# Attention with exponentiated scores as the stationary operand of the value product, plain fp32 loads with casts on GpSimd, and a hand-written order

## Chip, cores and metric

The kernel runs on one core of a Trainium2 chip. The metric is the device time of one execution in microseconds (us), taken as the median of several runs; every run quoted as fast lies within 1.5% of the fastest of its kernel. The profile is of one execution; its span is about 2 us shorter than the time of the same run.

## The reference

```python
q, k, v: float32 [8, 8, 512, 64]      # batch, heads, sequence, dim
scores = einsum('bhqd,bhkd->bhqk', q, k) / sqrt(64)
attn   = exp(scores - scores.max(-1)) ; attn = attn / attn.sum(-1)
out    = einsum('bhqk,bhkd->bhqd', attn, v)      # float32
```

There are 64 heads. Both kernels treat two at a time ("a pair", 32 in all), leave out the subtraction of the maximum (the exponent is of moderate size for these inputs), and get the sum for the normalization from a 65th column of ones beside the 64 of the values.

## The kernel before

The scores are computed transposed: 128 keys on the partitions, 512 queries along the free axis. "A half" below is half of a pair's work: two of its four key blocks, for both heads, which is two exponentials of 1,024 elements per partition. PSUM tiles are marked with the space that they take.

```python
q16, k16 = bt[b]                       # fp16; loaded a batch at a time by casting GpSimd DMAs
vp = apool.tile([P, 2, NI, D + 1], FP16, ...)            # values, and a column of ones
...                                    # 4 VectorE copies into qkp, two heads side by side
for i in range(NI):                    # 8 transposes into tqk_ps (2 KiB), one copy to tqk
    nc.tensor.transpose(tqk_ps[:, 0, i, :], qkp[:, 0, i, :], ident16)
    nc.tensor.transpose(tqk_ps[:, 1, i, :], qkp[:, 1, i, :], ident16)
...
for half in range(2):
    st_ps = [pspool.tile([P, 2, S], FP32, tag="ps_st", bufs=2, ...) for h01 in range(2)]   # 2 x 4 KiB
    for cc in range(2):
        for h01 in range(2):           # scores: 64 rows of the array for each head
            nc.tensor.matmul(st_ps[h01][:, cc, :], tqk[po:po+64, 1, c*P:(c+1)*P], tqk[po:po+64, 0, :], ...)
    for h01 in range(2):
        nc.scalar.activation(out=pt[h01][:, 2*half:2*half+2, :], in_=st_ps[h01][:, :, :], func=EXP, scale=scale)

ot_ps = [pspool.tile([P, S], FP32, tag="ps_ot", bufs=2, ...) for h01 in range(2)]          # 2 x 2 KiB
for h01 in range(2):
    for c in range(NI):                # values stationary (65 columns), exponentials moving (512)
        nc.tensor.matmul(ot_ps[h01][0:D+1, :], vp[:, h01, c, :], pt[h01][:, c, :], ...)
    nc.vector.tensor_copy(out=ot_sb[0:D+1, h01, :], in_=ot_ps[h01][0:D+1, :])
    op_ps = pspool.tile([P, NI, D + 1], FP32, tag="ps_outp", bufs=1, ...)                  # up to 2 KiB
    for c in range(NI):                # four fp32 transposes put the queries back on partitions
        nc.tensor.transpose(op_ps[:, c, :], ot_sb[0:D+1, h01, c*P:(c+1)*P], ident32[0:D+1, 0:D+1])
    ...                                # reciprocal of column 65, multiply, store on the sync queue
```

Counted in units of 2 KiB per partition, called banks below, the tiles above take 4 + 2 + 1 + 1 = 8 banks, 16 KiB.

The softmax here doesn't subtract the row's maximum and nothing guards it: scores larger than these inputs give would overflow.

## Time and profile before

| | before |
|---|---|
| time, median of 3 runs | 190.99 us (190.87 to 191.46) |
| span of the profile | 189.0 us |
| TensorE (PE) / ScalarE (ACT) / VectorE (DVE) busy | 88% / 66% / 61% |

In the page's second part each digit is the busy share of one of 40 slices of the span, in tenths:

```profile
PE   0057999999999999999999999999999999999980
ACT  2014388688786868686886868686877868686860
```

TensorE is at nine tenths or more from the fifth slice on, and ScalarE alternates between 6 and 8. (In these views PEld is TensorE's loading of stationary operands, POOL is GpSimd, and PEclk is the clock that TensorE was granted.) Groups of instructions are listed as line, engine, operation, output<-input, count, then busy time, mean ns of one, and the idle time just before it with what ended it. Two of TensorE's groups:

```profile
L110 PE MATMUL st<-tqk 64*128 64x512 f16 x256 | 65.6, 386 | 3.6 <-DVE tqk L98 0.8
...
L148 PE MATMUL outp<-ident,otsb 65*128 65x65 f32 x256 | 27.4, 229 | 3.2 <-DVE outsb L154 1.4
```

The second is the group of fp32 transposes that exist only because the value product leaves its output with queries on the free axis. The two DMA queues (packets, MB, share of 16 engines):

```profile
q0 software_dynamic: 50432, 12.59, 70.2%
q1 hardware_dynamic: 8704, 8.39, 12.8%
```

### The profile page before, as it was taken

Reading aid. Unit: us, or ns where it says so; the run is one execution under the profiler, and the core shown is the slowest. Engines: PE = TensorE matmul, PEld = TensorE weight load, DVE = VectorE, ACT = ScalarE, POOL = GpSimd, SP = SyncE. Lnnn points to the kernel's source line nnn. Section 1 sums busy time; section 2 is a strip of 40 time slices with the busy share of each in tenths; the row PEclk is TensorE's granted clock in tenths of the full one; section 3 lists DMA queues with packets and bytes.
Section 4 is the critical chain, followed back from the end, with each engine's and each line's share of the span. In section 5 each row is a group of like instructions: output and inputs, shape, how many; then the busy total and the mean of one; then the engine's idle time right before and its main releaser. Section 6 shows DMA issues by size and latency. Waiting matters only on the chain.

```text
span 189.0 us, 2952 instructions
## 1 busy us (share of the span) xinstructions
PE 166.8 (88%) x1024; PEld 74.9 (40%) x1024; DVE 115.1 (61%) x352; ACT 125.2 (66%) x129; POOL 66.5 (35%) x120
## 2 busy tenths in 40 slices
PE   0057999999999999999999999999999999999980
PEld 0033433434444343544353443434353443434330
DVE  0255455675859486666759585766757594656462
ACT  2014388688786868686886868686877868686860
POOL 7482643423453335413543336304133333300000
PEclk9999999999999999999999999999999999999999
DMA  3999999965599578995699478996555463631111
GB/s 42 191 182 183 129 156 189 179 87 77 65 147 196 80 91 111 182 170 83 86 143 188 74 91 126 179 149 87 83 83 76 34 90 67 87 69 59 55 57 55
DMA packets 59150, 21.16 MB, mean 112 GB/s; under 512 B 34560, under 2 KB 59136, under 8 KB 59136
## 3 DMA queue, kind: packets, MB, share of 16 engines
q0 software_dynamic: 50432, 12.59, 70.2%
q1 hardware_dynamic: 8704, 8.39, 12.8%
q8 instruction: 8, 0.13, 0.3%
q14 instruction: 6, 0.05, 0.1%
HBM read 25.17 MB, written 8.39 MB: 178 GB/s over the span
## 4 chain that ended last, share of the span: by engine, by line
PE 68%; DVE 11%; ACT 9%; DMA 6%; issue 2%; POOL 2%; ACTq 1%; POOLq 0%
PE st L110 31%; PE ot L131 31%; ACT pt L118 9%; DMA k<-in_k_dram 6%; DVE otsb L140 5%; DVE tqk L98 5%; PE outp L148 4%; PE tqkps L95 1%; POOL q L49 1%; ACTq L190 0%; POOL k L54 0%; DVE outsb L154 0%; DVE qkp L88 0%; POOL ident masks.py:199 0%; PE tqkps L96 0%
## 5 line engine op out<-in xcount | busy, mean ns | idle before, releaser
L118 ACT ACTIVATE pt<-st 128x1024 f16<-128x1024 f32 x128 | 124.0, 1024 | 56.8 <-PE st L110 56.8
L131 PE MATMUL ot<-pt,vp 128*65 128x512 f16 x256 | 73.4, 390 | 0.3 <-ACT pt L118 0.3
L140 DVE COPY otsb<-ot 65x512 f32<-65x512 f32 x64 | 43.8, 685 | 43.5 <-PE ot L131 43.5
L110 PE MATMUL st<-tqk 64*128 64x512 f16 x256 | 65.6, 386 | 3.6 <-DVE tqk L98 0.8
L77 POOL DMA_DIRECT2D vp<-in_v_dram x64 | 47.2, 743 | 14.4 <-POOL vp L75 9.6
L131 PEld LDWEIGHTS <-vp 128*65 128x65 f16 x256 | 21.9, 111 | 41.5 <-issue 33.9
L148 PEld LDWEIGHTS outp<-ident,otsb 65*128 65x128 f32 x256 | 23.4, 141 | 17.8 <-DVE otsb L140 9.3
L148 PE MATMUL outp<-ident,otsb 65*128 65x65 f32 x256 | 27.4, 229 | 3.2 <-DVE outsb L154 1.4
L75 POOL MEMSET vp<- 128x8 f16 x32 | 4.0, 139 | 70.6 <-PE ot L131 70.6
L95 PE MATMUL tqkps<-ident,qkp 128*128 128x128 f16 x128 | 21.0, 231 | 8.7 <-DVE qkp L84 7.6
L154 DVE TENSOR_TENSOR outsb<-outp,rcp 128x256 f32<-128x256 f32 x64 | 27.0, 422 | 1.3
L110 PEld LDWEIGHTS <-tqk 64*128 64x128 f16 x256 | 13.3, 94 | 25.7 <-issue 16.6
L96 PE MATMUL tqkps<-ident,qkp 128*128 128x128 f16 x128 | 20.9, 230 | 2.8 <-DVE qkp L88 2.8
L98 DVE COPY tqk<-tqkps 128x1024 f16<-128x1024 f16 x32 | 21.4, 670 | 0.5 <-PE tqkps L96 0.5
L84 DVE COPY qkp<-q 128x256 f16<-128x256 f16 x64 | 15.6, 256 | 8.4 <-DMA q<-in_q_dram 8.4
L153 DVE RECIPROCAL rcp<-outp 128x4 f32<-128x4 f32 x64 | 11.2, 175 | 14.5 <-PE outp L148 14.2
L95 PEld LDWEIGHTS <-qkp 128*128 128x128 f16 x128 | 12.8, 102 | 18.3 <-issue 7.6
L88 DVE COPY qkp<-k 128x256 f16<-128x256 f16 x64 | 16.4, 275 | 2.7 <-DMA k<-in_k_dram 2.7
L96 PEld LDWEIGHTS <-qkp 128*128 128x128 f16 x128 | 13.2, 103 | 6.9 <-DVE qkp L88 2.9
L49 POOL DMA_DIRECT2D q<-in_q_dram x8 | 7.2, 902 | 12.6 <-DVE qkp L88 9.2
L54 POOL DMA_DIRECT2D k<-in_k_dram x8 | 7.1, 892 | 0.1
L118 ACT ACT_TABLE_LOAD x1 | 1.3, 1283 | 0.7 <-PEq L179 0.7
(6 smaller groups left out, 1.3 us busy)
## 6 DMA issues: line engine op xcount, KB each, us to landing
out_dram<-outsb SPq DMA_DIRECT2D x32, 256.0 KB, 2.4
q<-in_q_dram POOLq DMA_DIRECT2D x8, 512.0 KB, 6.6
k<-in_k_dram POOLq DMA_DIRECT2D x8, 512.0 KB, 8.2
vp<-in_v_dram POOLq DMA_DIRECT2D x64, 64.0 KB, 3.1
```

Source lines behind the costliest of these rows:

```text
L77: nc.gpsimd.dma_start(out=vp[:, h01, :, 0:D], in_=v[b, hA + h01].rearrange("(p i) d -> p i d", i=NI),)
L84: nc.vector.tensor_copy(out=qkp[:, 0, :, 64 * h01 : 64 * h01 + 64], in_=q16[:, hA + h01, :].rearrange("p (i d) -> p i d", d=D),)
L88: nc.vector.tensor_copy(out=qkp[:, 1, :, 64 * h01 : 64 * h01 + 64], in_=k16[:, hA + h01, :].rearrange("p (i d) -> p i d", d=D),)
L95: nc.tensor.transpose(tqk_ps[:, 0, i, :], qkp[:, 0, i, :], ident16)
L96: nc.tensor.transpose(tqk_ps[:, 1, i, :], qkp[:, 1, i, :], ident16)
L98: nc.vector.tensor_copy(out=tqk[:, :, :], in_=tqk_ps[:, :, :, :])
L110: nc.tensor.matmul(st_ps[h01][:, cc, :], tqk[po : po + 64, 1, c * P : (c + 1) * P], tqk[po : po + 64, 0, :], start=True, stop=True,)
L118: nc.scalar.activation(out=pt[h01][:, 2 * half : 2 * half + 2, :], in_=st_ps[h01][:, :, :], func=EXP, scale=scale,)
L131: nc.tensor.matmul(ot_ps[h01][0 : D + 1, :], vp[:, h01, c, :], pt[h01][:, c, :], start=(c == 0), stop=(c == NI - 1),)
L140: nc.vector.tensor_copy(out=ot_sb[0 : D + 1, h01, :], in_=ot_ps[h01][0 : D + 1, :])
L148: nc.tensor.transpose(op_ps[:, c, :], ot_sb[0 : D + 1, h01, c * P : (c + 1) * P], ident32[0 : D + 1, 0 : D + 1],)
L154: nc.vector.tensor_tensor(out=out_sb[:, h01, :, :], in0=op_ps[:, :, 0:D], in1=rcp[:, h01, :].broadcast_to([P, NI, D]), op=AluOp.mult,)
```

## The change

Three things are changed at once. The value product is turned round, so that a 128x128 block of exponentials is the stationary operand and 65 columns of values move past it; queries then land on partitions, and the transposes back and their evictions go. The casting loads on GpSimd's queue become plain fp32 loads on the sync queue, with copies to fp16 on GpSimd. The order of instructions is written by hand, one pair ahead, in place of the framework's scheduler. The score buffers go from two to three, and the output from 2 + 1 PSUM tiles to one.

```diff
+    ps_st = ctx.enter_context(tc.tile_pool(name="ps_st", bufs=3, space=bass.MemoryType.PSUM))
+    ps_o = ctx.enter_context(tc.tile_pool(name="ps_o", bufs=1, space=bass.MemoryType.PSUM))
+    ps_t = ctx.enter_context(tc.tile_pool(name="ps_t", bufs=1, space=bass.MemoryType.PSUM))
 ...                                   (load: k, q and v of a pair, one transfer each)
-            nc.gpsimd.dma_start(
-                out=vp[:, h01, :, 0:D],
-                in_=v[b, hA + h01].rearrange("(p i) d -> p i d", i=NI),
+            nc.sync.dma_start(
+                out=t.rearrange("p h i d -> p h (i d)"),
+                in_=src[b, h : h + 2].rearrange("h (p i) d -> p h (i d)", i=NI),
             )
 ...                                   (cast: three per pair)
+            nc.gpsimd.tensor_copy(
+                out=t[:, n].rearrange("p i (h d) -> p h i d", h=2),
+                in_=tiles[name][:, :, :, :],
+            )
 ...                                   (values)
-            for c in range(NI):
-                nc.tensor.matmul(
-                    ot_ps[h01][0 : D + 1, :],
-                    vp[:, h01, c, :],
-                    pt[h01][:, c, :],
+        for qc in range(NI):
             for c in range(NI):
                 nc.tensor.matmul(
+                    o[:, qc, :],
+                    pts[g][h][:, c, qc * P : (qc + 1) * P],
+                    vps[g % NV][:, h, c, :],
                     start=(c == 0),
                     stop=(c == NI - 1),
                 )
-        for h01 in range(2):
-            nc.vector.tensor_copy(out=ot_sb[0 : D + 1, h01, :], in_=ot_ps[h01][0 : D + 1, :])
 ...                                   (fp32 transposes back: removed)
+    with tc.manual_schedule():
 ...                                   (5 pairs loaded, 3 cast)
+        for g in range(2):
+            transpose(g, 1)
+            transpose(g, 0)
+            if g == 0:
+                scores(0, 0)
+                scores(0, 1)
+        transpose(2, 1)
+        transpose(2, 0)
+        for g in range(NP):
+            load(g + AHEAD)
+            cast(g + 3)
+            scores(g + 1, 0)
+            values(g, 0)
+            transpose(g + 3, 1)
+            scores(g + 1, 1)
+            values(g, 1)
+            transpose(g + 3, 0)
```

More of the change, by code (lines that the diff above doesn't have):

```diff
@@ L4 @@
 import concourse.tile as tile
-from concourse import bass_utils, mybir
+from concourse import mybir
 from concourse._compat import with_exitstack
@@ L30 @@
     scale = float(D) ** -0.5
-    n_pairs = (B * H) // 2
+    NP = (B * H) // 2
     ppb = H // 2
-    cpool = ctx.enter_context(tc.tile_pool(name="att_const", bufs=1))
-    bpool = ctx.enter_context(tc.tile_pool(name="att_batch", bufs=2))
-    apool = ctx.enter_context(tc.tile_pool(name="att_a", bufs=4))
-    ppool = ctx.enter_context(tc.tile_pool(name="att_pair", bufs=3))
-    hpool = ctx.enter_context(tc.tile_pool(name="att_head", bufs=4))
-    opool = ctx.enter_context(tc.tile_pool(name="att_out", bufs=3))
@@ L41 @@
-    pspool = ctx.enter_context(tc.tile_pool(name="att_psum", bufs=1, space=bass.MemoryType.PSUM))
-    bt = {}
-    ident16 = None
-    ident32 = None
-    def batch_load(b):
-        q16 = bpool.tile([P, H, NI * D], FP16, tag="q16", name=f"q16_{b}")
-        nc.gpsimd.dma_start(
-            out=q16.rearrange("p h (i d) -> p h i d", d=D),
-            in_=q[b].rearrange("h (p i) d -> p h i d", i=NI),
-        )
-        k16 = bpool.tile([P, H, NI * D], FP16, tag="k16", name=f"k16_{b}")
-        nc.gpsimd.dma_start(
-            out=k16.rearrange("p h (i d) -> p h i d", d=D),
-            in_=k[b].rearrange("h (p i) d -> p h i d", i=NI),
-        )
-        bt[b] = (q16, k16)
@@ L60 @@
-    batch_load(0)
-    ident16 = cpool.tile([P, P], FP16, name="ident16")
-    make_identity(nc, ident16)
-    ident32 = cpool.tile([P, P], FP32, name="ident32")
-    make_identity(nc, ident32)
-    for g in range(n_pairs):
-        b = g // ppb
-        gl = g % ppb
-        hA = 2 * gl
-        if gl == 0 and b + 1 < B:
-            batch_load(b + 1)
-        q16, k16 = bt[b]
-        vp = apool.tile([P, 2, NI, D + 1], FP16, tag="vp", name=f"vp_{g}")
-        nc.gpsimd.memset(vp[:, :, :, D : D + 1], 1.0)
-        for h01 in range(2):
-            nc.gpsimd.dma_start(
-                out=vp[:, h01, :, 0:D],
-                in_=v[b, hA + h01].rearrange("(p i) d -> p i d", i=NI),
-            )
-        qkp = apool.tile([P, 2, NI, P], FP16, tag="qkp", name=f"qkp_{g}")
-        for h01 in range(2):
-            nc.vector.tensor_copy(
-                out=qkp[:, 0, :, 64 * h01 : 64 * h01 + 64],
-                in_=q16[:, hA + h01, :].rearrange("p (i d) -> p i d", d=D),
-            )
-            nc.vector.tensor_copy(
-                out=qkp[:, 1, :, 64 * h01 : 64 * h01 + 64],
-                in_=k16[:, hA + h01, :].rearrange("p (i d) -> p i d", d=D),
-            )
-        tqk_ps = pspool.tile([P, 2, NI, P], FP16, tag="ps_tqk", bufs=1, name=f"tqkps_{g}")
-        for i in range(NI):
-            nc.tensor.transpose(tqk_ps[:, 0, i, :], qkp[:, 0, i, :], ident16)
-            nc.tensor.transpose(tqk_ps[:, 1, i, :], qkp[:, 1, i, :], ident16)
-        tqk = ppool.tile([P, 2, S], FP16, tag="tqk", name=f"tqk_{g}")
-        nc.vector.tensor_copy(out=tqk[:, :, :], in_=tqk_ps[:, :, :, :])
-        pt = [hpool.tile([P, NI, S], FP16, tag="pt", name=f"pt_{g}_{h}") for h in range(2)]
-        for half in range(2):
-            st_ps = [
-                pspool.tile([P, 2, S], FP32, tag="ps_st", bufs=2, name=f"st_{g}_{h01}_{half}")
-                for h01 in range(2)
-            ]
-            for cc in range(2):
-                c = 2 * half + cc
-                for h01 in range(2):
-                    po = 64 * h01
-                    nc.tensor.matmul(
-                        st_ps[h01][:, cc, :],
-                        tqk[po : po + 64, 1, c * P : (c + 1) * P],
-                        tqk[po : po + 64, 0, :],
-                        start=True,
-                        stop=True,
-                    )
-            for h01 in range(2):
-                nc.scalar.activation(
-                    out=pt[h01][:, 2 * half : 2 * half + 2, :],
-                    in_=st_ps[h01][:, :, :],
-                    func=EXP,
-                    scale=scale,
-                )
-        ot_ps = [
-            pspool.tile([P, S], FP32, tag="ps_ot", bufs=2, name=f"ot_{g}_{h01}")
-            for h01 in range(2)
-        ]
-        for h01 in range(2):
@@ new lines @@
+    cpool = ctx.enter_context(tc.tile_pool(name="const", bufs=1))
+    lpool = ctx.enter_context(tc.tile_pool(name="load", bufs=6))
+    qpool = ctx.enter_context(tc.tile_pool(name="qk16", bufs=3))
+    tpool = ctx.enter_context(tc.tile_pool(name="tqk", bufs=4))
+    ppool = ctx.enter_context(tc.tile_pool(name="pt", bufs=6))
+    opool = ctx.enter_context(tc.tile_pool(name="out", bufs=4))
+    ps_st = ctx.enter_context(tc.tile_pool(name="ps_st", bufs=3, space=bass.MemoryType.PSUM))
+    ps_o = ctx.enter_context(tc.tile_pool(name="ps_o", bufs=1, space=bass.MemoryType.PSUM))
@@ new lines, with where, load @@
+    ps_t = ctx.enter_context(tc.tile_pool(name="ps_t", bufs=1, space=bass.MemoryType.PSUM))
+    NV = 6
+    vps = [cpool.tile([P, 2, NI, D + 1], FP16, name=f"vp{n}") for n in range(NV)]
+    ident = cpool.tile([P, P], FP16, name="ident")
+    raw = {}
+    qkp = {}
+    tqk = {}
+    st = {}
+    pts = {}
+    outs = {}
+    def where(g):
+        return g // ppb, 2 * (g % ppb)
+    def load(g):
+        if g >= NP:
+            return
+        b, h = where(g)
+        tiles = {}
+        for name, src in (("k", k), ("q", q), ("v", v)):
+            t = lpool.tile([P, 2, NI, D], FP32, tag=f"{name}32", name=f"{name}32_{g}")
+            nc.sync.dma_start(
+                out=t.rearrange("p h i d -> p h (i d)"),
+                in_=src[b, h : h + 2].rearrange("h (p i) d -> p h (i d)", i=NI),
+            )
+            tiles[name] = t
+        raw[g] = tiles
@@ new lines, in cast, with transpose @@
+    def cast(g):
+        if g >= NP:
+            return
+        tiles = raw.pop(g)
+        t = qpool.tile([P, 2, NI, P], FP16, tag="qkp", name=f"qkp_{g}")
+        for n, name in ((1, "k"), (0, "q")):
+            nc.gpsimd.tensor_copy(
+                out=t[:, n].rearrange("p i (h d) -> p h i d", h=2),
+                in_=tiles[name][:, :, :, :],
+            )
+        qkp[g] = t
+        nc.gpsimd.tensor_copy(out=vps[g % NV][:, :, :, 0:D], in_=tiles["v"][:, :, :, :])
+    def transpose(g, n):
+        if g >= NP:
+            return
+        if n == 1:
+            tqk[g] = tpool.tile([P, 2, S], FP16, tag="tqk", name=f"tqk_{g}")
+        tp = ps_t.tile([P, NI, P], FP16, tag="tp", name=f"tp_{g}_{n}")
+        for i in range(NI):
+            nc.tensor.transpose(tp[:, i, :], qkp[g][:, n, i, :], ident)
+        nc.vector.tensor_copy(out=tqk[g][:, n, :], in_=tp.rearrange("p i c -> p (i c)"))
@@ new lines, in scores @@
+    def scores(g, half):
+        if g >= NP:
+            return
+        if half == 0:
+            pts[g] = [
+                ppool.tile([P, NI, S], FP16, tag="pt", name=f"pt_{g}_{h}") for h in range(2)
+            ]
+        ss = [ps_st.tile([P, 2, S], FP32, tag="st", name=f"st_{g}_{h}_{half}") for h in range(2)]
+        for cc in range(2):
+            c = 2 * half + cc
+            for h in range(2):
+                po = 64 * h
+                nc.tensor.matmul(
+                    ss[h][:, cc, :],
+                    tqk[g][po : po + 64, 1, c * P : (c + 1) * P],
+                    tqk[g][po : po + 64, 0, :],
+                    start=True,
+                    stop=True,
+                )
+        for h in range(2):
+            nc.scalar.activation(
+                out=pts[g][h][:, 2 * half : 2 * half + 2, :],
+                in_=ss[h][:, :, :],
+                func=EXP,
+                scale=scale,
+            )
@@ L130, with values @@
+    def values(g, h):
+        if g < 0:
+            return
+        if h == 0:
+            outs[g] = opool.tile([P, 2, NI, D], FP32, tag="ob", name=f"ob_{g}")
+        ob = outs[g]
+        o = ps_o.tile([P, NI, D + 1], FP32, tag="o", name=f"o_{g}_{h}")
+        for qc in range(NI):
             for c in range(NI):
                 nc.tensor.matmul(
-                    ot_ps[h01][0 : D + 1, :],
-                    vp[:, h01, c, :],
-                    pt[h01][:, c, :],
+                    o[:, qc, :],
+                    pts[g][h][:, c, qc * P : (qc + 1) * P],
+                    vps[g % NV][:, h, c, :],
@@ L137 @@
                 )
-        ot_sb = opool.tile([P, 2, S], FP32, tag="ot_sb", name=f"otsb_{g}")
-        for h01 in range(2):
-            nc.vector.tensor_copy(out=ot_sb[0 : D + 1, h01, :], in_=ot_ps[h01][0 : D + 1, :])
-        out_sb = opool.tile([P, 2, NI, D], FP32, tag="out_sb", name=f"outsb_{g}")
-        rcp = opool.tile([P, 2, NI], FP32, tag="rcp", name=f"rcp_{g}")
-        for h01 in range(2):
-            op_ps = pspool.tile([P, NI, D + 1], FP32, tag="ps_outp", bufs=1,
-                                name=f"outp_{g}_{h01}")
-            for c in range(NI):
-                nc.tensor.transpose(
-                    op_ps[:, c, :],
-                    ot_sb[0 : D + 1, h01, c * P : (c + 1) * P],
-                    ident32[0 : D + 1, 0 : D + 1],
-                )
-            nc.vector.reciprocal(out=rcp[:, h01, :], in_=op_ps[:, :, D : D + 1])
-            nc.vector.tensor_tensor(
-                out=out_sb[:, h01, :, :],
-                in0=op_ps[:, :, 0:D],
-                in1=rcp[:, h01, :].broadcast_to([P, NI, D]),
-                op=AluOp.mult,
-            )
@@ L161 @@
-        nc.sync.dma_start(
-            out=out[b, hA : hA + 2].rearrange("h (p i) d -> p h (i d)", i=NI),
-            in_=out_sb[:, :, :, :],
-        )
+        rc = opool.tile([P, NI, 1], FP32, tag="rc", name=f"rc_{g}_{h}")
+        nc.vector.reciprocal(out=rc[:, :, :], in_=o[:, :, D : D + 1])
+        nc.vector.tensor_tensor(
+            out=ob[:, h],
+            in0=o[:, :, 0:D],
+            in1=rc[:, :, :].broadcast_to([P, NI, D]),
+            op=AluOp.mult,
+        )
+        if h == 1:
+            b, hh = where(g)
+            nc.sync.dma_start(
+                out=out[b, hh : hh + 2].rearrange("h (p i) d -> p h (i d)", i=NI),
+                in_=ob.rearrange("p h i d -> p h (i d)"),
+            )
+            del outs[g], pts[g]
@@ new lines @@
+    AHEAD = 5
+    with tc.manual_schedule():
+        for g in range(AHEAD):
+            load(g)
+        make_identity(nc, ident)
+        for n in range(NV):
+            nc.gpsimd.memset(vps[n][:, :, :, D : D + 1], 1.0)
+        for g in range(3):
+            cast(g)
+        for g in range(2):
[15 more added lines that the diff above has]
+            transpose(g + 3, 0)
```

## The prediction

> **What bounds the kernel now.** I read the page's busy shares first, then the chain that ended last, then the groups of instructions, the totals of waits, and last the timeline of two steady pairs of heads. Busy shares and chain of the page of before:
>
> ```profile
> PE 166.8 (88%) x1024; PEld 74.9 (40%) x1024; DVE 115.1 (61%) x352; ACT 125.2 (66%) x129; POOL 66.5 (35%) x120
> ...
> PE 68%; DVE 11%; ACT 9%; DMA 6%; issue 2%; POOL 2%; ACTq 1%; POOLq 0%
> ```
>
> TensorE owns 68% of the chain, ScalarE 9%, though ScalarE has 125 us of work in a span of 189. The groups say what that work is, and the waits say that ScalarE starves:
>
> ```profile
> L118 ACT ACTIVATE pt<-st 128x1024 f16<-128x1024 f32 x128 | 124.0, 1024 | 56.8 <-PE st L110 56.8
> L131 PE MATMUL ot<-pt,vp 128*65 128x512 f16 x256 | 73.4, 390 | 0.3 <-ACT pt L118 0.3
> L140 DVE COPY otsb<-ot 65x512 f32<-65x512 f32 x64 | 43.8, 685 | 43.5 <-PE ot L131 43.5
> L131 PEld LDWEIGHTS <-vp 128*65 128x65 f16 x256 | 21.9, 111 | 41.5 <-issue 33.9
> L148 PEld LDWEIGHTS outp<-ident,otsb 65*128 65x128 f32 x256 | 23.4, 141 | 17.8 <-DVE otsb L140 9.3
> L95 PEld LDWEIGHTS <-qkp 128*128 128x128 f16 x128 | 12.8, 102 | 18.3 <-issue 7.6
> ```
>
> ```profile
> ACT pt L118 <- PE st L110: 56.8, 50, 11.4
> ```
>
> Of 56.8 us that exponentials wait for scores, 11.4 is one wait at the start; the other 45 recur in the steady state. The timeline (start, duration, engine, line) shows why TensorE can't feed it:
>
> ```profile
> 103.36 0.38 PE L110 MATMUL st<-tqk 64*128 64x512 f16 x1
> 103.67 1.05 PE L131 MATMUL ot<-pt,vp 128*65 128x512 f16 x4
> 104.66 0.60 PE L110 MATMUL st<-tqk 64*128 64x512 f16 x2
> ...
> 105.64 0.41 PE L148 MATMUL outp<-ident,otsb 65*128 65x65 f32 x4
> ```
>
> Value products start 0.216 us apart. Each change between 64-row scores and 128-row work costs about 0.31 us from start to start (103.36 to 103.67); I count some 14 such breaks in 10.48 us, the steady period of two pairs (in the chain's listing the same exponential comes back at 90.46, 100.94 and 111.41). So a pair takes 5.24 us on TensorE, and four exponentials take only 4 x 0.912 = 3.65 us when fed: the group "106.69 2.86 ... x3" is 0.912 from start to start ((2.86 - 1.03)/2).
>
> [...]the fp16 load of 128 columns takes 102 ns, less than one of 65 columns (111), and the fp32 one of 128 takes 141. So a load of 128 fp16 columns occupies little.[...] The trace has no copy on GpSimd, only a 324 ns select of 128 elements.[...]
>
> **The change, part by part.**
> *Value product swapped.* 256 matmuls of 512 columns become 1,024 of 65 columns with the exponentials as weights, 32 per pair. The output lands with queries on partitions, so 256 fp32 transposes (27.4 us busy) and 64 VectorE evictions (43.8 us) go. A 512-column matmul costs 216 ns and a 128-column transpose 56 ns (109.22 to 109.28 in the timeline), i.e. 0.417 ns a column plus 2.5. At 65 columns that is 30 ns; with the weight load beside it I choose **35 ns**. 32 x 35 = 1.12 us replaces 8 x 216 + 8 x 62 = 2.22 us.
> *Order.* Each half pair is now: four scores, alternating heads, 16 values, four transposes; two breaks per half instead of three or four. TensorE per half:
> - scores: the alternated pairs run side by side, second pair 0.226 us after the first (0.60 - 0.376 for four in the trace);
> - break to values 0.31;
> - 16 values 0.56 plus 0.03 at the first;
> - from first to last transpose 3 x 0.056 = 0.17;
> - break back 0.27 (101.74 to 102.01).
> Sum **1.57 us**. ScalarE per half: 2 x 0.912 = **1.82 us**. ScalarE becomes the bound, TensorE has 0.25 us to spare.
> *Hand-over.* Three score buffers in place of two. The second tile of a half waits for the first exponential of the preceding half: that takes 1.02 us, the release some 0.1, then the first tile needs one more score and 0.47 us until ScalarE starts (100.46 to 100.94), ready at 1.59 us against the 1.82 at which ScalarE wants it. It holds, with 0.2 us in hand.
> *VectorE* per half: reciprocal 0.175, multiply 0.42, copy of 512 instead of 1,024 fp16 (0.67 now; some 0.40), about 1.03 us of 1.82. Its one output bank comes free about 0.98 us after the last value product; the next values start some 1.25 us after it. Hidden.
> *Loads.* 80 GpSimd-issued casting transfers go; 96 plain loads on the sync queue, 256 KB each, and 96 GpSimd copies come, 512 elements each.[...] Loads run five pairs ahead. Hidden, save at the start.
> *Start and end.* The first exponential now starts at 13.4 us (2.0 + 11.4). After: first load issued at 0.7, landed about 2.4 later (the store's median), two copies 1.6, transposes, two VectorE copies and scores 2.2: about **7.0 us**. Nine copies precede the second pair's scores, about 3.1 + 9 x 0.8 = 10.3, just when ScalarE finishes the first four (7.0 + 3.7). After the last exponential: values 0.9, normalization 0.7, store and closing 3.0, together 4.6 us (now 6.2).
> Sum: 7.0 + 128 x 0.912 (116.7) + 0.1 + 4.6 = 128.4 us of span; the median time lies 2.0 above the span now (191.0 against 189.0), so 130.4. For imperfect overlap and a ragged start I add 3: **133.5 us**, ratio 1.43.
>
> **Rivals.**
> *TensorE stays the bound.* If the small value products run at 60 ns rather than 35, as the fp32 transposes of 65 columns do now (62), a half is 1.97 us: 64 x 0.15 = 10 us more, 143. For it: every product needs its own weight load, and four in a row add to one bank. Against: the fast fp16 load above; the 62 ns goes with a slow fp32 load. At 45 ns the two engines tie.
> *GpSimd becomes the bound.* At 1.3 us a copy, three are 3.9 us a pair, 8 us more in all. For it: the select's 324 ns for 128 elements would scale to 1.3 us if all of it grew with size. Against: its fixed part is visible (98 ns for a memset of one element).
> *DMA becomes the bound.* The store queue now takes 12.8% of 16 engines for 32 stores: 0.128 x 189/32 = 0.76 us each. Four such transfers per pair are 3.0 us of 3.65, 83%, or 33.5 MB in 130 us = 258 GB/s[...]. If loads cost a quarter more per packet than stores it binds. I hold it unlikely, but loads then arrive with little slack in the first 10 us.
> *A wait in place of the removed one:* the hand-over has only 0.2 us of slack; 0.1 us lost per half would be 6 us.
> *Little gain because transfers or TensorE were hidden anyway:* refuted by 45 us of recurring ScalarE waits.
>
> **Range and chances.** Lower edge: all hidden and a faster start, 128.5. Upper edge: TensorE at 60 ns plus some start loss, 146. To lose the 2% gain, pairs would have to take over 5 us, more than any rival here gives. Faster 0.97, same 0.02, slower 0.01.
>
> **What would show it.** Right: the chain mostly ScalarE exponentials; ScalarE busy above 90% of slices; exponentials 0.91 us apart; weight loads of the value product near 100 ns and its matmuls some 35 ns apart; first exponential near 7 us. Wrong: exponentials still waiting for scores for over 10 us after the start (TensorE or hand-over); transposes waiting for GpSimd copies; GpSimd copies waiting for loads. The number is wrong above all if the spacing of the 65-column products is near 60 ns or a GpSimd copy takes over 1.2 us.

## The result, and the profile after

| | before | after |
|---|---|---|
| time, median of fast runs | 191.23 us (190.87 to 191.87, 4 runs) | 135.98 us (135.73 to 136.24, 4 runs) |
| span of the profile | 189.0 us | 134.3 us |
| first exponential starts | 13.4 us | 7.50 us |
| exponentials, steady state, start to start | waits recur | 0.914 to 0.917 us on average |

The ratio is 0.7115, with a 95% interval of 0.7092 to 0.7138. Ratios throughout are the mean time of one kernel's fast runs over that of the other's fast runs of the same rounds, so they are not quite the ratio of the medians quoted. Results are correct.

Busy shares, slices, sync queue and chain of the page after (the chain is followed back from the last instruction, and says what the end hung on):

```profile
PE 115.7 (86%) x1536; PEld 61.6 (46%) x1536; DVE 60.4 (45%) x192; ACT 118.9 (89%) x129; POOL 59.9 (45%) x108
...
PE   0475999999999999999999999999999999998750
...
ACT  3073599999999999999999999999999999999930
...
q1 hardware_dynamic: 34816, 33.56, 78.7%
...
ACT 64%; issue 15%; PE 12%; DVE 3%; DMA 2%; POOL 0%; ACTq 0%
```

ScalarE's row is full from the sixth slice on, and it has taken over the chain, 64% against 9%. TensorE's row is nearly as full, yet TensorE isn't the bound; a busy share doesn't tell the two apart, the chain and the waits do. The groups and the wait:

```profile
L115 ACT ACTIVATE pt<-st 128x1024 f16<-128x1024 f32 x128 | 117.6, 1261 | 9.0 <-PE st L107 9.0
...
L131 PEld LDWEIGHTS <-pt 128*128 128x128 f16 x1024 | 36.6, 99 | 28.5 <-DVE tqk L93 24.6
L131 PE MATMUL o<-vp,pt 128*128 128x65 f16 x1024 | 44.5, 196 | 1.6 <-DVE ob L140 1.6
L78 POOL CAST qkp<-k 128x512 f16<-128x512 f32 x32 | 19.6, 613 | 48.8 <-DMA k<-in_k_dram 33.5
```

```profile
ACT pt L115 <- PE st L107: 9.0, 3, 5.5
```

Exponentials wait for scores three times in the whole run, 9.0 us, instead of 50 times and 56.8 us. All three waits lie before 17 us. The mean duration of an exponential grew from 1,024 to 1,261 ns, but that isn't the rate: records of neighbours overlap. 128 of them have 117.6 us as their union, 0.92 each. When one engine is the bound, read the distance between starts, not the mean of the durations. (Why the records lengthen was not examined.)

A steady half, from the timeline (start, duration, engine, line, operation, count):

```profile
59.53 4.04 ACT L115 ACTIVATE pt<-st 128x1024 f16<-128x1024 f32 x4
...
60.48 0.69 PE L131 MATMUL o<-vp,pt 128*128 128x65 f16 x16
...
61.00 0.39 PE L92 MATMUL tp<-ident,qkp 128*128 128x128 f16 x4
...
61.32 1.06 PE L107 MATMUL st<-tqk 64*128 64x512 f16 x4
...
62.31 0.68 PE L131 MATMUL o<-vp,pt 128*128 128x65 f16 x16
```

One half runs from 60.48 to 62.31, 1.83 us, and ScalarE needs 2 x 0.917 = 1.83. The group of four scores is 1.06 long where 0.60 would do: after its first score TensorE waits until ScalarE has released a score buffer (from 61.32 to 61.79, about 0.47 us). TensorE has slack, and the third buffer is what that slack goes through.

The start is less smooth. First ScalarE, then TensorE, after:

```profile
7.50 3.77 ACT L115 ACTIVATE pt<-st 128x1024 f16<-128x1024 f32 x4 [5.48 <-PE st L107]
14.43 1.94 ACT L115 ACTIVATE pt<-st 128x1024 f16<-128x1024 f32 x2 [3.15 <-PE st L107]
```

```profile
9.52 0.61 PE L92 MATMUL tp<-ident,qkp 128*128 128x128 f16 x4
10.64 0.59 PE L92 MATMUL tp<-ident,qkp 128*128 128x128 f16 x4 [0.51 <-DVE tqk L93]
11.74 0.59 PE L92 MATMUL tp<-ident,qkp 128*128 128x128 f16 x4 [0.51 <-DVE tqk L93]
12.84 0.59 PE L92 MATMUL tp<-ident,qkp 128*128 128x128 f16 x4 [0.51 <-DVE tqk L93]
13.36 1.03 PE L107 MATMUL st<-tqk 64*128 64x512 f16 x4
```

The fourth exponential starts at 10.23, and the fifth only at 14.43: 4.20 us instead of 0.92, so 3.3 are lost. In between TensorE transposes pairs 1 and 2 in full, four blocks through one PSUM bank, the last three each waiting 0.51 us for VectorE to empty it, before it makes the next score. Four transposes take 0.59 us here against 0.39 in the steady half above: they start 107 ns apart, not 56. **TensorE still runs at half rate.** The trace's record of the full clock begins at 16.5 us.

### The profile page after: what moved, and what is told of

It reads as the page before. It is cut to its first block, busy times and chain, and to the rows that moved or that the text cites. A ratio compares the mean times of both kernels' runs of the same rounds, so it can differ in the third digit from the quotient of the medians.

```text
span 134.3 us, 3901 instructions
## 1 busy us (share of the span) xinstructions
PE 115.7 (86%) x1536; PEld 61.6 (46%) x1536; DVE 60.4 (45%) x192; ACT 118.9 (89%) x129; POOL 59.9 (45%) x108
## 4 chain that ended last, share of the span: by engine, by line
ACT 64%; issue 15%; PE 12%; DVE 3%; DMA 2%; POOL 0%; ACTq 0%
ACT pt L115 64%; PE st L107 5%; PE o L131 3%; PE tp L92 3%; DMA k<-in_k_dram 2%; DVE tqk L93 2%; DVE ob L140 1%; POOL qkp L78 0%; DVE rc L139 0%; ACTq L115 0%
## 5 line engine op out<-in xcount | busy, mean ns | idle before, releaser
L115 ACT ACTIVATE pt<-st 128x1024 f16<-128x1024 f32 x128 | 117.6, 1261 | 9.0 <-PE st L107 9.0
L131 PEld LDWEIGHTS <-pt 128*128 128x128 f16 x1024 | 36.6, 99 | 28.5 <-DVE tqk L93 24.6
L131 PE MATMUL o<-vp,pt 128*128 128x65 f16 x1024 | 44.5, 196 | 1.6 <-DVE ob L140 1.6
L78 POOL CAST qkp<-k 128x512 f16<-128x512 f32 x32 | 19.6, 613 | 48.8 <-DMA k<-in_k_dram 33.5
L139 DVE RECIPROCAL rc<-o 128x4 f32<-128x4 f32 x64 | 11.6, 182 | 57.1 <-PE o L131 57.1
L93 DVE COPY tqk<-tp 128x512 f16<-128x512 f16 x64 | 26.4, 413 | 11.3 <-PE tp L92 11.3
L92 PE MATMUL tp<-ident,qkp 128*128 128x128 f16 x256 | 26.1, 228 | 6.3 <-POOL qkp L78 4.2
L140 DVE TENSOR_TENSOR ob<-o,rc 128x256 f32<-128x256 f32 x64 | 27.1, 424 | 2.2
L83 POOL CAST vp<-v 128x512 f16<-128x512 f32 x32 | 19.7, 616 | 5.8 <-DMA v<-in_v_dram 3.9
L78 POOL CAST qkp<-q 128x512 f16<-128x512 f32 x32 | 19.6, 613 | 2.5 <-DMA q<-in_q_dram 1.9
L92 PEld LDWEIGHTS <-qkp 128*128 128x128 f16 x256 | 16.5, 101 | 7.8 <-POOL qkp L78 4.7
```

Of the source, the lines that this page charges most:

```text
L78: nc.gpsimd.tensor_copy(out=t[:, n].rearrange("p i (h d) -> p h i d", h=2), in_=tiles[name][:, :, :, :],)
L83: nc.gpsimd.tensor_copy(out=vps[g % NV][:, :, :, 0:D], in_=tiles["v"][:, :, :, :])
L92: nc.tensor.transpose(tp[:, i, :], qkp[g][:, n, i, :], ident)
L93: nc.vector.tensor_copy(out=tqk[g][:, n, :], in_=tp.rearrange("p i c -> p (i c)"))
L115: nc.scalar.activation(out=pts[g][h][:, 2 * half : 2 * half + 2, :], in_=ss[h][:, :, :], func=EXP, scale=scale,)
L131: nc.tensor.matmul(o[:, qc, :], pts[g][h][:, c, qc * P : (qc + 1) * P], vps[g % NV][:, h, c, :], start=(c == 0), stop=(c == NI - 1),)
```

## The experiments

The theory to begin with was the prediction's: TensorE's work was cut below ScalarE's, so ScalarE sets the time, and most of that comes from turning the product round. The rivals: the transfers bind wherever the old loads are kept (their shares of time looked like 83% of a longer span); the gain is really the third score buffer; the gain is really the hand-written order. All kernels gave correct results except one that is marked.

| kernel | median us of fast runs | ratio to before (95% interval) |
|---|---|---|
| e1: before, product turned round only | 240.28 | 1.2559 (1.2522 to 1.2597) |
| e1b: e1 with three score buffers | 144.78 | 0.7583 (0.7546 to 0.7621) |
| e3: after, with the old loads | 143.21 | 0.7473 (0.7444 to 0.7502) |
| e4: after, with two score buffers | 181.79 | 0.9483 (0.9444 to 0.9521) |
| e9: after, order left to the scheduler | 136.08 | 0.7109 (0.7087 to 0.7131) |
| e10: e1 with 32 dummy matmuls at the fifth pair | 176.19 | 0.9254 (0.9192 to 0.9316) |
| e12: before, third score buffer squeezed in | 413.85 | 2.1656 (2.1595 to 2.1716) |
| e5 / e6: after, value product done twice / thrice | 143.88 / 176.94 | 0.7533 / 0.9261 |
| e8: after, exponentials on half the columns (wrong) | 123.04 | 0.6405 (0.6365 to 0.6445) |
| e7: after, other start order | 134.03 | 0.7009 (0.6986 to 0.7033) |
| e11: e7, TensorE kept busy early, last store split | 131.83 | 0.6887 (0.6868 to 0.6906) |

### e1: the turned product alone

```diff
-                nc.tensor.matmul(ot_ps[h01][0 : D + 1, :], vp[:, h01, c, :], pt[h01][:, c, :], ...)
-            nc.vector.tensor_copy(out=ot_sb[0 : D + 1, h01, :], in_=ot_ps[h01][0 : D + 1, :])
-                nc.tensor.transpose(op_ps[:, c, :], ot_sb[0 : D + 1, h01, ...], ident32[...])
+            for qc in range(NI):
+                for c in range(NI):
+                    nc.tensor.matmul(op_ps[:, qc, :], pt[h01][:, c, qc * P : (qc + 1) * P], vp[:, h01, c, :], ...)
```

The output takes two banks here, the scores keep two buffers, loads and order stay as before.

> The kernel before with the value product swapped and nothing else (old casting loads, two score buffers, scheduled order). Theory: TensorE is relieved as in the change, but the old casting loads were 70.2% of 189 us = 132.7 us and the stores 24 us of all 16 DMA engines, so the DMA engines become the bound: 158 to 172 us, DMA near 90% busy and waits on loads. Rival A, the swap alone carries the gain: 135 to 145 us. Rival B, the order and the third buffer carry it: 175 us or more with exponentials waiting for scores.

This was a clear miss of the theory and of rival A: 240.28 us, a quarter slower than before. It lies in rival B's open range (175 or more), which didn't name a slowdown. Page of e1, then its timeline on TensorE:

```profile
PE 219.3 (92%) x1536; PEld 96.6 (41%) x1536; DVE 81.1 (34%) x288; ACT 132.0 (55%) x129; POOL 66.2 (28%) x118
...
PEclk9999999999999999999999999999999999999999
...
L108 PE MATMUL st<-tqk 64*128 64x512 f16 x256 | 128.9, 617 | 2.6 <-ACT pt L116 1.8
```

```profile
122.82 0.31 PE L93 MATMUL tqkps<-ident,qkp 128*128 128x128 f16 x1
122.93 0.31 PE L94 MATMUL tqkps<-ident,qkp 128*128 128x128 f16 x1
...
123.39 1.03 PE L108 MATMUL st<-tqk 64*128 64x512 f16 x2
124.35 1.06 PE L130 MATMUL outp<-vp,pt 128*128 128x65 f16 x16
```

A score takes 617 ns (386 before), transposes start 107 ns apart (56 in before's steady state), and 16 value products span 1.06 us against 0.69 after. TensorE does everything at half rate, for the whole run; a half takes 3.445 us. The page's clock row says 9 throughout: the trace of e1 holds no clock record at all, and the row shows full speed where there is none. Kernels before and after have the same half rate at their start. Before's TensorE, from the timeline of its start:

```profile
17.58 0.31 PE L95 MATMUL tqkps<-ident,qkp 128*128 128x128 f16 x1
17.69 0.31 PE L96 MATMUL tqkps<-ident,qkp 128*128 128x128 f16 x1
...
19.36 2.68 PE L131 MATMUL ot<-pt,vp 128*65 128x512 f16 x8
```

Transposes lie 0.11 us apart up to the first long run of eight 512-column value products at 19.36; from about 21 us on they lie 56 ns apart. The last gap in TensorE's records ends 3.6 us before the full clock begins, in before (17.41 and 20.99 us) as in after (12.84 and 16.46); in e11, below, it ends about 5.2 us before (1.45 and 6.7). E1 shows no such change: TensorE is 92% busy by its records and stays at half rate for all of its 238 us. What ends the half rate is not shown.

### e1b: the same with three score buffers

```diff
-                pspool.tile([P, 2, S], FP32, tag="ps_st", bufs=2, name=f"st_{g}_{h01}_{half}")
+                pspool.tile([P, 2, S], FP32, tag="ps_st", bufs=3, name=f"st_{g}_{h01}_{half}")
-            op_ps = pspool.tile([P, NI, D + 1], FP32, tag="ps_outp", bufs=2,
+            op_ps = pspool.tile([P, NI, D + 1], FP32, tag="ps_outp", bufs=1,
```

> The swapped value product in the kernel before, as in the run that did it alone, with three score buffers (the output banks give one up). Theory A: the half-rate clock of TensorE is what made the swap alone slow, and a third buffer doesn't change the broken order: 205 us or more, products 54 ns apart. Theory B: two buffers were the cause: below 160 us, products 33 ns apart.

It took 144.78 us, span 142.4, with full rate from 22.7 us on and a half of 1.877 us on average. The third buffer, for which the output gives up one of its two banks here, is worth 95 us beside the turned product. E1b, with the old loads and the scheduler's order, is already within 9 us of the whole change. Of the two expectations the one that had e1b stay slow fell.

### e10: is the half rate of e1 a state that one push ends?

```diff
+        if g == 4:
+            wps = pspool.tile([P, S], FP32, tag="ps_warm", bufs=1, name="wps")
+            for m in range(32):
+                nc.tensor.matmul(wps[:, :], tqk[:, 1, 0:P], tqk[:, 0, :], start=(m == 0), stop=(m == 31))
```

> The swapped value product alone, plus 32 dummy matmuls of 512 columns at the fifth pair, most of them back to back. Theory (the clock has two stable states): the dense stretch lifts TensorE to its full rate[...], and it stays there: products 33 ns apart afterwards, 150 to 185 us. Rival (the mix of work decides): it falls back to half rate within some us, and the run ends at 240 us plus up to 14 for the dummies.

It took 176.19 us: 32 useless matmuls at the fifth pair save 64 us. They did not run as one stretch, though. By the timeline nine of them lie between 31.58 and 41 us, in groups of one to four among other work, and the clock record of full rate begins at 40.8 us; the run of eighteen follows only at 44.31. So the full rate did not come from that long dense run of dummies. From the timeline of e10, long after that:

```profile
104.00 0.61 PE L137 MATMUL outp<-vp,pt 128*128 128x65 f16 x14
104.54 0.60 PE L115 MATMUL st<-tqk 64*128 64x512 f16 x2
```

Two scores take 0.60 us, not e1's 1.03, and value products lie 33 ns apart; the full rate lasts from 40.8 us to 170.5, where TensorE's work ends. So e1's loop can run on at either rate, once in it. That is shown for this execution; what decides between the rates isn't. Of e10's four runs, one of 179.69 us is slow and isn't in the median or the ratio. That run and the one of 177.37 us have mean clocks of 0.956 and 0.955, against 0.989 in the profiled one. If the difference is time at half rate, it is an estimated 12 us (0.034 x 175 / 0.5), so there the full rate probably lapsed for a while.

Full rate with two buffers still gives a half of 2.164 us, against e1b's 1.877. The buffers therefore matter in themselves as well: of the 95 us between e1 and e1b, 64 go with the rate in e10, and the rest isn't separated further.

### e4: the change, with two score buffers

```diff
-    ps_st = ctx.enter_context(tc.tile_pool(name="ps_st", bufs=3, space=bass.MemoryType.PSUM))
+    ps_st = ctx.enter_context(tc.tile_pool(name="ps_st", bufs=2, space=bass.MemoryType.PSUM))
```

> The changed kernel with two score buffers instead of three. Theory (hand-over): the second tile of a half waits for the exponential just running, so each half costs two exponentials (1.94 us from first start to second end) plus release 0.05 plus one score and start 0.48 = 2.47 us instead of 1.83: 64 x 0.64 = 41 us more, 172 to 182 us. Rival, the third buffer is slack that TensorE never needed: 134 to 140 us.

It took 181.79 us, as expected, 46 more than with three. The total of waits in e4, and ScalarE's timeline:

```profile
ACT pt L115 <- PE st L107: 47.2, 64, 5.4
```

```profile
50.91 1.94 ACT L115 ACTIVATE pt<-st 128x1024 f16<-128x1024 f32 x2 [0.54 <-PE st L107]
53.33 1.94 ACT L115 ACTIVATE pt<-st 128x1024 f16<-128x1024 f32 x2 [0.48 <-PE st L107]
```

After each two exponentials ScalarE waits about half a microsecond: with two buffers TensorE can't make the next scores while both are being read, so the two engines take turns. A half is 2.42 us in these lines (2.480 in the median). On top of that the clock goes up and down (0.837 in the mean); this trace does have clock records, 18, and the page's row for e4 is:

```profile
PEclk9999999985899698895799798589969759995555
```

At half rate, between 80.6 and 87.4 us by the clock records, ScalarE's waits are longer:

```profile
81.53 1.94 ACT L115 ACTIVATE pt<-st 128x1024 f16<-128x1024 f32 x2 [0.76 <-PE st L107]
84.26 1.94 ACT L115 ACTIVATE pt<-st 128x1024 f16<-128x1024 f32 x2 [0.79 <-PE st L107]
```

A half is 2.73 there, and 2.42 to 2.48 in the stretches at full rate. So most of the 46 us is the buffers and not the clock: about 64 x (2.45 - 1.83) = 40 us, an estimate from these figures. In the page's row for TensorE the four slices at clock 5 before the last four of the span are busy at 9, and those at clock 9 from the sixth on at 7 or 8.

### e12: the third buffer without the turned product

The old product with three score buffers would need 6 + 2 + 1 + 1 = 10 banks. It was squeezed into the 8 of before: one ot tile instead of two, and both kinds of transposes through one shared bank.

```diff
-        tqk_ps = pspool.tile([P, 2, NI, P], FP16, tag="ps_tqk", bufs=1, ...)
+        tqk_ps = pspool.tile([P, 2, NI, P], FP16, tag="ps_sh", bufs=1, ...)
-                pspool.tile([P, 2, S], FP32, tag="ps_st", bufs=2, ...)
+                pspool.tile([P, 2, S], FP32, tag="ps_st", bufs=3, ...)
-            pspool.tile([P, S], FP32, tag="ps_ot", bufs=2, ...)
+            pspool.tile([P, S], FP32, tag="ps_ot", bufs=1, ...)
-            op_ps = pspool.tile([P, NI, D + 1], FP32, tag="ps_outp", bufs=1, ...)
+            op_ps = pspool.tile([P, NI, D + 1], FP32, tag="ps_sh", bufs=1, ...)
```

> The kernel before with a third score buffer and the old value product; the two banks that it costs are taken from the old product (one output bank instead of two, and the query/key transposes and the output transposes share one). Theory: the gain needs the swapped product, which takes work from TensorE and gives the banks for the third buffer; with the old product TensorE keeps its work and now also waits for evictions through single banks: 185 us or more. Rival: the third buffer alone, which ended the half-rate clock and the waits of the swapped product, is the change's whole gain: below 160 us.

The direction was as expected, but 413.85 us is far more than the theory reckoned with. From the waits of e12:

```profile
ACT pt L118 <- PE st L110: 280.5, 32, 12.3
```

The single banks put the stages of a pair one behind the other, and TensorE's records look like half rate for the whole run: a score takes 618 ns on average (617 in e1, 386 in before), and transposes start 0.11 us apart at 211 us. So the run shows that a third buffer bought this way is worthless; a third buffer for the old product without the squeeze was not built, and its worth stays open.

### e3: the change, with the old loads

```diff
-            nc.gpsimd.tensor_copy(...)          # three casts per pair, from fp32 loads on the sync queue
+            nc.gpsimd.dma_start(...)            # q16, k16 a batch at a time, v a head at a time, casting
+                nc.vector.tensor_copy(...)      # four copies per pair into qkp, as before
```

> The changed kernel with the old loads put back (casting DMAs issued by GpSimd, q and k by batch, VectorE copies into the pair layout). Theory: 157 us of DMA work can't be hidden under 118 us of exponentials: 158 to 172 us, loads waited for throughout. Rival, transfers are hidden anyway and GpSimd casts were only a convenience: 134 to 140 us.

A second miss: 143.21 us, not 158 or more, and just above the rival's 134 to 140. The queues of e3:

```profile
q0 software_dynamic: 50432, 12.59, 95.1%
q1 hardware_dynamic: 8704, 8.39, 20.9%
```

Together these come to 116% of 16 engines' time, which no occupancy can be. Packets' times overlap, and this share isn't a capacity; the rival that took it for one falls. In e3's steady state a half is 1.830 us, the same as after. What differs is the start: the first exponential starts at 14.36 us instead of 7.50. That is 6.9 of the 7.2 us between the two medians. The new loads are worth the start, and nothing else.

### e9: the change, order left to the scheduler

```diff
-    with tc.manual_schedule():
+    if True:
```

> The changed kernel with the framework's scheduler instead of the hand-written order. It keeps the coarse order but does the two scores of one head after one another instead of alternating heads, which costs TensorE 3 x 0.215 instead of 0.226 us per half, i.e. 0.42 us more of the 0.46 that the trace of after leaves idle. Theory: it still fits or just misses, 135 to 142 us. Rival, the hand-written order carries much of the gain: 150 us or more.

It took 136.08 us against 135.98, and 1.825 us a half. The order by hand is worth nothing where ScalarE is the bound. (What the source says first, one pair ahead, is still there for the scheduler to work from.)

### e5 and e6: how much slack does TensorE have?

```diff
-            for c in range(NI):
+            for m in range(2 * NI):             # e6: 3 * NI
+                c = m % NI
```

Each product is done twice or thrice, and since the ones column is too, the normalized result is still right.

> The changed kernel with every value product done twice into the same sum (numerator and denominator double alike, so the result stays right). Measures TensorE's slack per half pair. By the prediction's sum TensorE takes 1.57 us of 1.82, so 0.52 more makes 2.09: 64 x 0.26 = 17 us more, 152 us. By the trace of after (1.37 without waits, and 0.94 instead of 0.88 from a last value product to the next first one because the output bank must be normalized first) it is 1.95: 7 us more, 143 us. If TensorE were already the bound: 64 x 0.52 = 33 us more, 169 us.

> As the run with every value product twice, but three times. By the trace of after 2.48 us per half: 41 us more, 177 us, and 34 us over the run with two. By the prediction's sum 2.62: 51 us more, 187 us. The difference of the two runs measures one set of 16 products at 64 x 0.52 = 34 us if TensorE bounds both.

Doubling the product's 16 matmuls per half costs only 7.9 us, tripling 41. E5's waits, and its TensorE timeline:

```profile
PEld L132 <- DVE ob L141: 29.5, 61, 0.9
```

```profile
58.14 1.19 PE L132 MATMUL o<-vp,pt 128*128 128x65 f16 x32
59.17 0.39 PE L92 MATMUL tp<-ident,qkp 128*128 128x128 f16 x4
59.49 0.61 PE L107 MATMUL st<-tqk 64*128 64x512 f16 x4
```

In e5 the bound is TensorE together with the single output bank: the next values wait for VectorE's multiply. A half is 1.930 us (1.95 expected from the trace after, 2.09 if the prediction's sum had been true). From e5 to e6 another 33.1 us come, over 64 halves 0.517 us, or 32 ns for each of 16 products: the cost of one where nothing hides it. In after itself the first 0.52 us added per half are thus paid with 0.1; about 0.4 us of each half was slack.

### e8: what comes after ScalarE?

```diff
-                out=pts[g][h][:, 2 * half : 2 * half + 2, :],
-                in_=ss[h][:, :, :],
+                out=pts[g][h][:, 2 * half : 2 * half + 2, 0 : S // 2],
+                in_=ss[h][:, :, 0 : S // 2],
```

The other half of the exponentials is a constant of ones, so the result is wrong (relative error 0.56); all other engines do the same work.

> Wrong result on purpose: each exponential covers half of its columns (the rest of its tile holds ones), so ScalarE needs some 0.49 us instead of 0.92 per tile. Shows what bounds next. If TensorE's 1.37 to 1.43 us per half is next: 64 x 1.43 + 18 = 106 to 111 us. If the 16 DMA engines are next (their packets took 105.7 us of all engines in the run of after): 114 to 120 us. If ScalarE's issue or the hand-over is: above 120.

It took 123.04 us (one of the four runs, 125.11 us, is slow and left out), with a half of 1.422 us in the median. From its timeline:

```profile
60.41 1.09 ACT L113 ACTIVATE ptc<-st 128x512 f16<-128x512 f32 x2 [0.34 <-PE st L105]
...
61.72 0.56 PEld L129 LDWEIGHTS <-ptc 128*128 128x128 f16 x16 [0.47 <-DVE ob L138]
...
61.84 1.09 ACT L113 ACTIVATE ptc<-st 128x512 f16<-128x512 f32 x2 [0.34 <-PE st L105]
```

ScalarE now waits for scores in every half, and TensorE for the output bank. So ScalarE was the bound after; TensorE with its one output bank comes next, 0.41 us a half below. The whole time, which falls in the expectation's third range (above 120 us), is less telling: six memsets of the constant on VectorE delayed the start to 16.18 us, 8.7 us later than in after. A few waits for loads appear too (the chain has 19% DMA): at this pace they are no longer all hidden.

### e7: another order at the start

```diff
-        for g in range(2):
-            transpose(g, 1)
-            transpose(g, 0)
-            if g == 0:
-                scores(0, 0)
-                scores(0, 1)
-        transpose(2, 1)
-        transpose(2, 0)
+        transpose(0, 1); transpose(0, 0); scores(0, 0)
+        transpose(1, 1); scores(0, 1); transpose(1, 0)
+        load(AHEAD); cast(3)
+        scores(1, 0); transpose(2, 1); values(0, 0); transpose(2, 0)
+        scores(1, 1); transpose(3, 1); values(0, 1); transpose(3, 0)
-        for g in range(NP):
+        for g in range(1, NP):
```

> The changed kernel with a new prologue alone: the transposes of the second pair lie between the scores of the first, the second pair's scores come before the third pair's transposes. Theory: the wait of 3.3 us before the fifth exponential came from four serial blocks of transpose and copy (1.1 us each through one bank), so it goes: 132.5 to 133.5 us. Rival, GpSimd casts or loads set that start: same as the change, 136.

It took 134.03 us, 1.95 less than after, where 2.5 to 3.5 were expected: the direction held, the size was missed. Two gaps of note remain, before the exponentials at 11.84 and 14.66 us, and both fall before 15.1 us, while TensorE is at half rate. All gaps together come to 1.7 us, against 3.7 in after. The order of the start was thus a little over half of its raggedness; e11 shows that the rate was the rest.

### e11: both kernels beaten

```diff
+    def heat(n):                       # dummy 512-column matmuls into the output bank, on a tile of ones
+        ...
+        nc.vector.memset(warm, 1.0)
+        heat(7)
 ...
         transpose(0, 1)
+        heat(2)
         transpose(0, 0)
+        heat(2)
         scores(0, 0)
 ...                                    and the last pair's store is split by head
```

> The new prologue, dummy matmuls while TensorE waits for the first loads (so that it leaves half rate earlier) and the last store split by head. Theory: the first exponential starts some 0.5 us earlier and the end comes 0.4 us earlier than with the prologue alone: 131.5 to 132.5 us. Rival, the first loads set the start whatever the clock: as the prologue alone.

It took 131.83 us, the fastest of all. Its ScalarE timeline:

```profile
7.56 13.86 ACT L116 ACTIVATE pt<-st 128x1024 f16<-128x1024 f32 x15 [5.55 <-PE st L108]
```

Fifteen exponentials without a gap, from the first on; TensorE is at full rate from 6.7 us by the clock record, against 15.1 in e7; with the dummies its records have no gap from 1.45 us on, where it had only the loads to wait for. Of the 2.2 us against e7, 1.7 are e7's gaps and 0.4 the tail (5.14 us from the last exponential's end to the end of the span, against 5.50 in e7). The time was in the expected range, but one of its two reasons was not: the first exponential starts at 7.56 us, against 7.63 in e7, and not 0.5 us earlier.

## Why the prediction was right, and where it wasn't

The time, the range and the direction held (133.5 in 128.5 to 146.0, against 135.98).

**ScalarE becomes the bound:** right. The chain is 64% ScalarE, three waits instead of fifty, a half of 1.83 us against 1.82 predicted, and e8 shows the next bound well below.

**The sum**, term by term, on the span: the first exponential started at 7.50 (7.0); from the first to the last start 119.84 us, of which 3.72 were gaps at the start (an allowance of 3) and the remaining 116.12 over 127 steps are 0.914 each (0.912); the last exponential ended at 128.66; the tail was 5.65 (4.6). Time minus span was 1.7 (2.0). The largest mis-sized term is the tail. From the timeline of the end of after:

```profile
127.99 0.67 PE L131 MATMUL o<-vp,pt 128*128 128x65 f16 x16 [0.82 <-DVE ob L140]
...
129.40 1.06 PE L131 MATMUL o<-vp,pt 128*128 128x65 f16 x16 [0.73 <-DVE ob L140]
```

The last values wait 0.73 us for the one output bank, which the sum forgot: where the exponentials end, the bank is no longer hidden behind them. They then run at half rate again, 1.06 instead of 0.67 us.

**The ragged start** was foreseen as a size, with the wrong cause. The prediction had the nine casts finish at 10.3 us, just in time. Each takes 0.61 us instead of 0.8 (the estimate, which no trace of before shows), but they wait for loads in between and the ninth ends at 11.46; nothing before the fifth exponential's score waited for that. The prediction missed four blocks of transposes through one bank before this score, and the half rate. E7 and e11 show the two shares.

**TensorE per half**, 1.57 us: too high. Products lie 33 ns apart (35), but the break back to scores is 0.15 rather than 0.27, and the whole comes to about 1.42 us with the output bank (e8). Harmless, since ScalarE hides it; it did make the expected penalty of e5 and e6 from that sum too large by 8 to 10 us.

**The hand-over** with three buffers holds, and it was named as the place where a wait could come. How much hangs on it was not seen: e4 loses 46 us without the third buffer. The prediction counted the work that the turned product takes from TensorE, and not the two PSUM banks that it sets free. Both count: turned alone, e1 lost 49 us to before, and even with the full rate for most of its span (e10) gained only 15; with the third buffer, e1b gained 46.

**The clock** is what the prediction didn't consider at all. Its rates were all read in the steady state of before, at full rate, and it took for granted that the changed kernel would reach it. After does, at 16.5 us; e1, which differs from e1b by one score buffer more and one output bank fewer in e1b, doesn't. The figure was right partly because the change brought the third buffer with it; that this also brought the full rate was luck, as far as the prediction goes.

**The DMA rival** was put aside, rightly, but on a comparison of a share of packets' time with capacity that e3 shows to be meaningless, and that made e1 and e3's expectations wrong. One of the signs that the prediction named for being wrong did appear: GpSimd copies waited for loads, 33.5 us for k alone in the group above. It cost nothing after the start, since no exponential waited after 17 us.

**Slips in the working** that changed nothing: by its own sum the two engines tie at 51 ns a product and not at 45 (1.57 + 16 x 0.016 = 1.82), the timeline of before has 12 breaks in 10.48 us and not 14, and (2.86 - 1.03)/2 is 0.915, where the starts in the trace give 0.912.

**The parts of the 55 us**, as the experiments allow: the turned product and the third buffer that it makes room for, together, 46 us (before to e1b, each in its own rounds); the loads 7 us, all at the start; the hand-written order alone nothing measurable; the rest, about 1.6 us between e1b and e3, lies within what else differs between those two.

**Left open:** what sets TensorE's rate, and why e1 stays at half rate at 92% busy; what a third score buffer would do for the old product; why exponentials' records lengthen without their rate changing.

## What to carry to other kernels

When a change removes work from the bounding engine, look as well at which buffers it frees: here the freed PSUM banks decided between a quarter slower and a quarter faster (e1 1.2559, e1b 0.7583), in part by way of the clock. Read rates from the distance between starts of neighbours, at the start and in the steady state, and check with them that TensorE is at full rate, because neither a busy share nor a clock row that has no records will say so (e1: 92% busy and 9 throughout, with transposes 107 ns apart). In e11, where the first matmuls wait for loads anyway, 5.1 us of dummy matmuls left the first exponential where it was (7.56 us, 7.63 in e7), and they took part in the last 2.2 us gained.
